# Issuing the last convolution, output weight and query stores on ScalarE's queue instead of SyncE's

## The chip, the cores and the metric

The kernel runs on one core of a Trainium2 chip. The metric is the time of one execution in microseconds, measured on the device; the median of several runs is quoted. The engines are named as in the profile: PE (TensorE matmul), PEld (TensorE weight load), DVE (VectorE), ACT (ScalarE), POOL (GpSimd), SP (SyncE, which only issues DMAs here; "SPq" in the rows). PEclk is the clock that TensorE was granted, as a share of 2.4 GHz.

## What is computed

One block of a hybrid encoder, in f32, on a sequence of 2048 rows of 1024 numbers. Cut to what matters here:

```python
xn = rms_norm(h, ln_mix_g)
proj = xn @ w_in                       # q, k, v, o, gates, c_q, c_kv, k_rope
qk = silu(dwconv3_centred(concat(q_pre, k_pre), conv_w, conv_b))
y_a = sigmoid(o_pre) * rms_norm(mlstm_fwd(qk, v, gates) + mlstm_bwd(qk, v, gates))
q = (rms_norm(c_q) @ w_uq)             # 4 heads: 128 plain and 64 rotated columns
o = softmax((q_nope @ k_nope.T + rope(q_rope) @ rope(k_rope).T) * scale) @ v
h = h + concat(y_a, y_b) @ w_out
h = h + conv_gated_mlp(rms_norm(h)); h = h + gate * rms_norm(p @ w_p)
out = rms_norm(h)
```

## The kernel before, in words

The kernel runs its stages one after another on a PE that is hardly ever without work; every intermediate goes to DRAM and comes back. All DMAs, loads and stores alike, are issued by SP, which works through one list in order: a DMA whose data are not ready holds up every DMA behind it. The framework gives each tile its semaphores and puts the instructions of each engine into an order of its own, by a simulated timetable in which program order is the priority; an instruction may therefore stand far ahead of the place where it is written. Only PE's order in the query stage is kept as written (`manual_schedule`).

Four stages matter, with their times in the profiled execution.

- **pairs** (to 424 us): `pairs()` runs 12 products, i = 0 to 11, each for two 128-column tiles of `w_in` and half the rows (`s.blk`), with seven partial products each (L544). `conv(s, half)` follows in the next iteration: for `s.pr` up to 3 it makes the depthwise convolution and Silu of a q or k tile and stores it to `qk_d`, else it makes the output gate and stores it to `o_d` (both stores are L576, 512 KB each). After i = 10 the corrected edge column is stored (L682). `queries_load` and `queries_begin` already fetch the next stage's weights during i = 10 and 11, among them the rotation tables of row blocks 0 and 1 (`load_table`, L749, tile `qcs`, tags t0 to t3).
- **queries** (424 to 482 us): `queries()` walks row blocks b = 0 to 3 of 512 rows. `rope(b)` makes two products `qpr`, rotates them on DVE (L815 to L817), splits the result into a high and a low part (`qso`: ACT casts, DVE subtracts) and stores it per head with four DMAs of 256 KB (L823). `latent(b, h)` makes the plain part of head h, ACT copies it to `qo` (L832), and one DMA stores it (L833). `weights(h)` folds a value weight into `w_out` (`woo`, copied by ACT at L799 and stored by two DMAs at L800). `split_c`, `split_wo` and `split_latent` make high and low parts of later operands (ACT casts, DVE subtracts). The tiles are reused: `qso` lies in two places by turns of b, `qo` in two by turns of head pairs, `woo` in two; so a copy into one waits until the earlier store from there has been read out.
- **attention's beginning**, woven into the queries: `attend_begin` loads the queries of the first 2 x 256 rows of head 0 back from `q_d` (`load_q`, L1162, tile `q_t`), splits them (ACT, then DVE), and starts the scores (L1155, tile `bk`, one PSUM bank for 512 keys, of which there are four that `rope`, `latent` and `weights` also use), the maximum (DVE L1184) and the exponential (ACT L1201). It is resumed at b = 1, 2 and 3.
- **attention and mLSTM** (482 to 1130 us) and then the MLP and gate stages (to the end), which the change does not touch.

The two lines that decide the order between queries and attention:

```python
if b == 1:
    att = self.attend_begin()
    next(att)                 # load_q(0, 0), load_q(0, 1)
if b > 1:
    next(att)                 # b = 2: split_q(0, 0)
```

Of the kernel before, what the change touches and what calls it, by code (L numbers as in the profile page):

```python
# [19 lines left out]
P = 128  # L20
# [15 lines left out]
SB = 512  # L36
# [12 lines left out]
def _f(ap):  # L49
    return ap.bitcast(F32)  # L50
# [10 lines left out]
class Block:  # L61
# [444 lines left out]
    def pairs(self):  # L506

        nc, d = self.nc, self.d
# [39 lines left out]
        def conv(s, half):  # L548
            u = s.u[half]
            if s.pr > 3:  # L550
                h = 2 * (s.pr - 4) + half
                nc.scalar.activation(u[:, 1 + SB:1 + 2 * SB], u[:, 1 + SB:1 + 2 * SB], AF.Sigmoid)
                t = self.at(("w7", "w11")[half], [P, 2 * SB], name="ct")
                nc.scalar.activation(t, u[:, 1:1 + 2 * SB], AF.Copy, scale=go[:, h:h + 1])
                dst = self.o_d[8 * s.blk:8 * s.blk + 8, :, h, :]
            else:
                ch = 2 * s.pr + half
                nc.vector.memset(u[:, 1 + 2 * SB:2 + 2 * SB], 0.0)
                if s.blk:
                    nc.vector.tensor_copy(u[:, 0:1], edge[:, ch:ch + 1])  # L560
                else:
                    nc.vector.memset(u[:, 0:1], 0.0)
                t = self.at(("w7", "w11")[half], [P, 2 * SB], name="ct")
                nc.scalar.activation(t, u[:, 0:2 * SB], AF.Identity, bias=cwt[:, 3, ch:ch + 1], scale=cwt[:, 0, ch:ch + 1])
                for tap in (1, 2):
                    nc.vector.scalar_tensor_tensor(t, u[:, tap:tap + 2 * SB], cwt[:, tap, ch:ch + 1], t,
                                                   op0=ALU.mult, op1=ALU.add)
                if s.blk:
                    nc.vector.scalar_tensor_tensor(part[:, ch:ch + 1], u[:, 1:2], cwt[:, 2, ch:ch + 1],
                                                   part[:, ch:ch + 1], op0=ALU.mult, op1=ALU.add)  # L570
                else:
                    nc.scalar.copy(edge[:, ch:ch + 1], u[:, 2 * SB:2 * SB + 1])
                    nc.scalar.copy(part[:, ch:ch + 1], t[:, 2 * SB - 1:2 * SB])
                nc.scalar.activation(t, t, AF.Silu)
                dst = self.qk_d[8 * s.blk:8 * s.blk + 8, :, ch, :]
            nc.sync.dma_start(dst.rearrange("c p t -> p c t"), t.rearrange("p (c t) -> p c t", t=P))  # L576

        def first_half(s, half, src):
            o = s.u[half][:, 1:1 + SB]
# [21 lines left out]
        for i in range(12):  # L601
            blk, j = divmod(i, 6)
            then = i == 5
            s = Pair()
            s.i, s.pr, s.blk, s.ops = i, j, blk, self.ops.pop(i)
            x, s.y = [self.pfa.tile([P, SB], F32, name=t, tag=t) for t in ("fx", "fy")]
            s.z, s.spare = [self.pfb.tile([P, SB], F32, name=t, tag=t) for t in ("fz", "fs")]
            s.u = [None, None]

            def side(at):  # L610
                if i == 0 and at == 1:
                    next(self.begun)
                if i == 0 and at in (2, 3):
                    for k in (2 * at - 4, 2 * at - 3):
                        self.xop["T3"][k] = self.in_place(0, "T3", k)
                        self.split(self.third[at - 2][:, k % 2], *self.xop["T3"][k])
                if i == 0 and at in (5, 6):
                    load("T4", range(2))
                if i == 1 and at in (1, 2):
                    load("B22", range(2))  # L620
                if (1, 4) < (i, at) < (5, 0) and at % 2:
                    self.gate_bank = prev.spare if at % 2 else s.spare
                    next(gates, None)
                if i == 11:
                    self.queries_begin(at, prev.spare if at % 2 else s.spare)

            if i < 2:
                op = self.xop["B11"][0]
                nc.tensor.matmul(s.y, s.ops["A11"][0][:, 0:P], op[0], start=True, stop=True)
            prod(x, s.ops["A11"], "B11")  # L630
            nc.scalar.copy(s.y, x)
            if then:
                load("B11")
            side(1)
            prod(s.z, s.ops["S1"], "T1")
            s.p5 = self.at("t6", [P, SB], name="p5")
            nc.scalar.copy(s.p5, s.z)
            if then:
                load("T1")
            side(2)  # L640
            if prev:
                rest_y(prev)
            if i == 6:
                load("T4")
            side(3)
            prod(s.y, s.ops["S2"], "T2", True)
            s.u[0] = self.at(next(urot), [P, 2 * SB + 2], name="ug")
            nc.scalar.copy(s.u[0][:, 1 + SB:1 + 2 * SB], s.y)
            if then:
                load("T2")  # L650
            side(4)
            if i + 1 < 12:
                for _ in self.pair_prep(i + 1):
                    pass
            if i + 2 < 12:
                self.pair_load(i + 2)
            if i == 10:
                self.queries_load()
            prod(x, s.ops["A12"], "B21", True)
            first_half(s, 0, x)  # L660
            side(5)
            if prev:
                rest_z(prev)
            if i == 6:
                load("B22")
            side(6)
            if then:
                load("B21")
            prod(s.y, s.ops["S3"], "T3", True)
            s.u[1] = self.at(next(urot), [P, 2 * SB + 2], name="uv")  # L670
            add(s.u[1][:, 1 + SB:1 + 2 * SB], s.p5, s.y)
            if then:
                load("T3")
            side(7)
            if i == 4:
                begin(1, self.NAMES)
            prev = s
            if i == 4:
                assert next(gates, 0) == 0
            if i == 10:  # L680
                nc.scalar.activation(part, part, AF.Silu)
                nc.sync.dma_start(self.qk_d[7, :, :, P - 1], part)  # L682
        rest_z(prev)
        rest_y(prev)

# [22 lines left out]
    def queries_begin(self, at, bank):  # L708

        nc = self.nc  # L710
        if at in (2, 4):
            kt = at // 2 - 1
            ps = bank.rearrange("p (h c) -> p h c", h=NH)
            for h in range(NH):
                nc.tensor.matmul(ps[:, h], self.uq[:, h, kt * P:(kt + 1) * P], self.uk[:, h], start=True, stop=True)
            nc.scalar.copy(self.wqr[kt][:, 0:512], bank)
        if at == 1:
            self.raws, self.tables = {}, {}
            self.first = self.at("x11", [P, 2, 2, SB], name="qraw")
            for b in range(2):  # L720
                self.load_latent(b)
                self.load_table(b)
        if at == 3:
            self.kraw = []
            for n in range(2):
                self.load_keys(n)
        if at == 5:
            self.wo = [self.split_wo(0)]
        if at == 6:
            self.kh, self.kl = self.split_latent(0, ("x12", "x13"))  # L730
# [36 lines left out]
    def queries(self):  # L767

        nc, d = self.nc, self.d
# [22 lines left out]
        def weights(h):  # L792
            (wh, wl), us = self.wo[h]
            for hf in range(2):
                fs = slice(hf * 512, hf * 512 + 512)
                ps = self.bank() if h else self.gbank()
                self.mm3(ps, us[:, 0], us[:, 1], wh[:, fs], wl[:, fs], True, True)
                o = self.at(("t6", "u2")[hf], [P, 512], name="woo")
                nc.scalar.copy(o, ps)  # L799
                nc.sync.dma_start(self.wo_d[h, :, fs], o)  # L800

        def product(ps, b, o):
            hi, lo = cc[b]
# [3 lines left out]
        def rope(b):  # L807
# [12 lines left out]
                self.split(t[2 * n], so[:, 0, n], so[:, 1, n])  # L820
            for h in range(NH):
                dst = self.q_d[h, 1, :, b * SB:(b + 1) * SB].rearrange("(a f) t -> f a t", a=4)
                nc.sync.dma_start(dst, _f(so[32 * h:32 * h + 32]).rearrange("p a n t -> p (a n) t"))  # L823
            if b < 2:
                self.load_table(b + 2)

        def latent(b, h):
            if h % 2 == 0:
                self.qo = self.at(f"u{h // 2}", [P, 2, SB], name="qo")
            ps = (self.bank if h % 2 and b < 3 else self.gbank)()  # L830
            product(ps, b, h * P)
            nc.scalar.activation(self.qo[:, h % 2], ps, AF.Copy, scale=ASCALE)  # L832
            nc.sync.dma_start(self.q_d[h, 0, :, b * SB:(b + 1) * SB], self.qo[:, h % 2])  # L833

        with self.tc.manual_schedule(engines={mybir.EngineType.PE}):
            split_wq()
# [1544 lines left out]
```

## Time and profile before

| | |
|---|---|
| median of 3 runs | 2837.93 us (2836.57 to 2844.72) |
| profiled execution, its own time | 2839.65 us |
| profiled execution, span first to last instruction | 2837.5 us |
| PE busy | 2803.8 us, 99% |
| DVE busy | 2123.0 us, 75% |
| ACT busy | 1573.2 us, 55% |
| DMA | 553.73 MB, mean 195 GB/s |

The span is what lies between the first and the last instruction of the profile; the execution's own time is 2.2 us longer. DMA-issuing instructions are in the timeline (SPq), with the time for which they occupied their queue, but are not counted as busy. The DMA share of a stretch is the mean busy share of the core's 16 DMA engines. A row of a timeline gives start, duration, engine, line, operation, tiles, count, and in brackets how long the engine had stood idle and on what. All DMAs of the kernel run on one queue, "q1 hardware_dynamic"; no row shows ACT issuing one.

### The profile page before, as it was taken

To read this page: it belongs to the slowest core of one execution; us is meant where nothing else is said; L and a number is where in the kernel's file an instruction comes from. 1 tells how busy PE (TensorE), PEld (TensorE's weight loads), DVE (VectorE), ACT (ScalarE), POOL (GpSimd) and SP (SyncE) were. 2 spreads that over 40 slices of the span, in tenths; PEclk is the share of its full clock that TensorE was granted. 3 is DMA by queue.
4 is the path that set the end of the run, shared out by engine and by line. 5 is a ranking of instruction groups with operands and counts; after the bars stand their busy time and mean duration, and the time that the engine had idled before them with its cause. 6 is when DMAs were issued, how large, how long until landed. Compare 5 with 4: busy or idle time off the path is not lost.

```text
span 2837.5 us, 39455 instructions
## 1 busy us (share of the span) xinstructions
PE 2803.8 (99%) x13756; PEld 2349.8 (83%) x13756; DVE 2123.0 (75%) x3597; ACT 1573.2 (55%) x3068; POOL 211.2 (7%) x331
## 2 busy tenths in 40 slices
PE   9999999999999999999999999999999999999998
PEld 8888887888888888888888888888888788888787
DVE  4867866778777777877778778777778766676777
ACT  6346775556565556655655556655556332254665
POOL 2100000000000000045100000000000000011012
PEclk9999999999999999999999999999999999999999
DMA  8874757654443333589645445567776757585864
GB/s 295 291 238 117 219 180 217 193 171 143 137 129 107 99 99 126 161 258 284 225 156 193 163 163 186 185 208 237 227 238 216 225 194 236 171 265 200 292 200 164
DMA packets 444207, 553.73 MB, mean 195 GB/s; under 512 B 34500, under 2 KB 294632, under 8 KB 444008
## 3 DMA queue, kind: packets, MB, share of 16 engines
q1 hardware_dynamic: 444008, 551.21, 60.2%
q8 instruction: 108, 1.77, 0.3%
q14 instruction: 91, 0.75, 0.1%
HBM read 358.50 MB, written 192.61 MB: 194 GB/s over the span
## 4 chain that ended last, share of the span: by engine, by line
PE 87%; DVE 4%; DMA 3%; ACT 1%; issue 1%; SPq 0%; POOL 0%; POOLq 0%; ACTq 0%; DVEq 0%
PE fy L1729 22%; PE fz L1729 15%; PE fx L1729 14%; PE bk L1155 9%; PE ppv L1236 6%; PE tb L1251 4%; PE fy L544 3%; PE bk L134 2%; PE fz L544 2%; PE fx L544 2%; PE fs L134 2%; PE mb L1117 1%; PE mb L1022 1%; PE mb L1118 1%; DMA opr<-tw_d 1%
## 5 line engine op out<-in xcount | busy, mean ns | idle before, releaser
L1729 PE MATMUL fz<-op,fw 128*128 128x512 f32 x1968 | 477.4, 391 | 2.7 <-DVE ug L1714 2.0
L1729 PE MATMUL fy<-op,fw 128*128 128x512 f32 x1968 | 475.2, 390 | 1.6 <-DVE xt L1714 1.6
L1729 PE MATMUL fx<-op,fw 128*128 128x512 f32 x1968 | 476.2, 390 | 0.0
L1729 PEld LDWEIGHTS fy<-op,fw 128*128 128x128 f32 x1968 | 368.6, 188 | 78.7 <-DVE xt L1714 2.0
L1729 PEld LDWEIGHTS fz<-op,fw 128*128 128x128 f32 x1968 | 367.4, 188 | 80.1 <-DVE ug L1714 2.5
L1729 PEld LDWEIGHTS fx<-op,fw 128*128 128x128 f32 x1968 | 368.1, 188 | 76.2
L1155 PE MATMUL bk<-kv,q_t 128*128 128x512 f32 x1280 | 337.4, 404 | 5.2 <-DVE q_t L124 4.0
L1155 PEld LDWEIGHTS bk<-kv,q_t 128*128 128x128 f32 x1280 | 230.3, 190 | 48.9 <-DVE q_t L124 4.4
L121 ACT CAST pt<-tb 128x512 fp32r<-128x512 f32 x256 | 139.7, 588 | 184.0 <-PE tb L1251 183.8
L1729 PE MATMUL fy<-op,fwd 128*128 128x512 f32 (+1 forms) x984 | 238.0, 390 | 2.5 <-DVE fh L1714 1.6
L1184 DVE TENSOR_REDUCE mx<-bk 128x1 f32<-128x512 f32 x256 | 174.8, 686 | 60.7 <-PE bk L1155 57.9
L1729 PEld LDWEIGHTS fy<-op,fwd 128*128 128x128 f32 x984 | 182.6, 188 | 41.5 <-DVE fh L1714 1.9
L1236 PE MATMUL ppv<-pt,kv 128*128 128x512 f32 (+1 forms) x1024 | 198.7, 344 | 1.0 <-DVE pt L124 1.0
L1201 ACT ACTIVATE pe<-bk,nm 128x512 f32<-128x512 f32 x256 | 174.2, 697 | 36.7 <-DVE nm L1195 36.4
L124 DVE TENSOR_TENSOR pt<-tb,pt 128x512 fp32r<-128x512 f32 x256 | 167.8, 684 | 32.3 <-ACT pt L121 30.5
L124 DVE TENSOR_TENSOR fw<-fwr,fw 128x1024 fp32r<-128x1024 f32 x124 | 150.9, 1220 | 34.5 <-ACT fw L121 34.3
L1236 PEld LDWEIGHTS ppv<-pt,kv 128*128 128x128 f32 x1024 | 156.0, 189 | 20.4 <-DVE pt L124 1.5
L121 ACT CAST op<-opr 128x512 fp32r<-128x512 f32 x201 | 116.9, 618 | 74.4 <-DMA opr<-tw_d 13.3
L121 ACT CAST fw<-fwr 128x1024 fp32r<-128x1024 f32 x124 | 129.8, 1051 | 37.4 <-DVE fwr L1703 20.2
L124 DVE TENSOR_TENSOR op<-opr,op 128x512 fp32r<-128x512 f32 x201 | 131.5, 690 | 25.4 <-ACT op L121 23.8
L1251 PE MATMUL tb<-ident,pe 128*128 128x128 f32 x1024 | 135.2, 273 | 0.1
L121 ACT CAST fw<-hraw 128x1024 fp32r<-128x1024 f32 (+1 forms) x72 | 70.1, 980 | 114.7 <-PE fx L1729 59.1
(397 smaller groups left out, 4443.2 us busy)
## 6 DMA issues: line engine op xcount, KB each, us to landing
fwr<-in_w_up SPq DMA_DIRECT2D x66, 512.0 KB, 4.9
fh<-h_d SPq DMA_DIRECT2D x48, 512.0 KB, 4.1
h_d<-fh SPq DMA_DIRECT2D x48, 512.0 KB, 4.5
s_d<-fwr SPq DMA_DIRECT2D x44, 512.0 KB, 3.4
fws<-s_d SPq DMA_DIRECT2D x44, 512.0 KB, 3.6
rw<-row_d SPq DMA_DIRECT2D x32, 512.0 KB, 4.9
tw_d<-tsum SPq DMA_DIRECT2D x60, 256.0 KB, 5.3
opr<-tw_d SPq DMA_DIRECT2D x60, 256.0 KB, 4.4
```

The source lines that it names most:

```text
L121: nc.scalar.copy(hi, src)
L124: (sub or nc.vector).tensor_tensor(lo, src, _f(hi), op=ALU.subtract)
L134: mm = lambda *a, **k: self.nc.tensor.matmul(*a, **k, skip_group_check=more)
L544: nc.tensor.matmul(out, a[:, k * P:(k + 1) * P], parts[lo], start=first, stop=lo == 1 and k == 3, skip_group_check=more)
L1022: mm(ps[:, i, 0:129], kw[:, h, :], v1[:, h, :], start=True, stop=True)
L1117: mm(ps[:, i, 0:129], mk2[:, r, h, :], v1[:, h, :], start=True, stop=False)
L1155: mm = lambda *a, **k: self.chained(nc.tensor.matmul(*a, **k))
L1184: nc.vector.tensor_reduce(s.mx[:, kb:kb + 1], ps, axis=AX.X, op=ALU.max)
L1201: nc.scalar.activation(s.pe[:, kb % 2], s.banks[kb], AF.Exp, bias=s.nm, accum_out=s.rs[:, kb:kb + 1])
L1236: mm = lambda *a, **k: self.chained(nc.tensor.matmul(*a, **k))
L1251: self.chained(nc.tensor.transpose(t[:, j, :], s.p[kb][:, j * P:(j + 1) * P], self.ident))
L1729: nc.tensor.matmul(out, a[:, k * P:(k + 1) * P], parts[lo][:, cols], start=first, stop=lo == 1 and k == last, skip_group_check=more)
```

## The change

The stores of `conv` for i = 9, 10 and 11 (six), the edge column's store, the eight stores of `woo`, the sixteen of `qso` and the sixteen of `qo` are issued by ACT, 47 in all; everything else stays with SP. The loads of the first two rotation tables are written at i = 9 instead of in `queries_begin` at i = 11.

```diff
@@ conv @@
-            nc.sync.dma_start(dst.rearrange("c p t -> p c t"), t.rearrange("p (c t) -> p c t", t=P))
+            issue = nc.scalar if s.i > 8 else nc.sync
+            issue.dma_start(dst.rearrange("c p t -> p c t"), t.rearrange("p (c t) -> p c t", t=P))
@@ pairs @@
             if i + 2 < 12:
                 self.pair_load(i + 2)
+            if i == 9:
+                self.raws, self.tables = {}, {}
+                for b in range(2):
+                    self.load_table(b)
...
                 nc.scalar.activation(part, part, AF.Silu)
-                nc.sync.dma_start(self.qk_d[7, :, :, P - 1], part)
+                nc.scalar.dma_start(self.qk_d[7, :, :, P - 1], part)
@@ queries_begin @@
         if at == 1:
-            self.raws, self.tables = {}, {}
             self.first = self.at("x11", [P, 2, 2, SB], name="qraw")
             for b in range(2):
                 self.load_latent(b)
-                self.load_table(b)
@@ queries: weights, rope, latent @@
-                nc.sync.dma_start(self.wo_d[h, :, fs], o)
+                nc.scalar.dma_start(self.wo_d[h, :, fs], o)
...
-                nc.sync.dma_start(dst, _f(so[32 * h:32 * h + 32]).rearrange("p a n t -> p (a n) t"))
+                nc.scalar.dma_start(dst, _f(so[32 * h:32 * h + 32]).rearrange("p a n t -> p (a n) t"))
...
-            nc.sync.dma_start(self.q_d[h, 0, :, b * SB:(b + 1) * SB], self.qo[:, h % 2])
+            nc.scalar.dma_start(self.q_d[h, 0, :, b * SB:(b + 1) * SB], self.qo[:, h % 2])
```

## Rows read from the trace of the kernel before

**Rows 1.** The page, part 1: busy time of each engine.

```profile
PE 2803.8 (99%) x13756; PEld 2349.8 (83%) x13756; DVE 2123.0 (75%) x3597; ACT 1573.2 (55%) x3068; POOL 211.2 (7%) x331
```

**Rows 2.** Waits of PE, whole span: total us, times, longest.

```profile
PE bk L1155 <- DVE q_t L124: 4.0, 1, 4.0
PE mb L1022 <- DVE kk L1015: 2.3, 1, 2.3
...
PE bk L1155 <- ACT pe L1201: 1.2, 2, 1.0
```

**Rows 3.** Busy by stretch; after ACT and POOL: granted clock, DMA share, GB/s.

```profile
454.00:458.00 4.00, 0.62 (x3) 0.19 (x1) 0.00 (x0) 2.86 (x7) 0.00 (x0) 0.90 1.03 341
458.00:460.00 2.00, 1.35 (x3) 1.16 (x4) 0.76 (x2) 0.44 (x2) 0.00 (x0) 0.50 1.02 339
...
462.00:464.00 2.00, 2.00 (x7) 1.52 (x6) 0.68 (x1) 0.00 (x0) 0.00 (x0) 0.50 0.99 382
...
507.00:510.00 3.00, 0.69 (x6) 0.66 (x6) 2.56 (x5) 1.28 (x3) 0.00 (x0) 1.00 0.80 272
```

**Rows 4.** Chain that ended last, in order of time, ahead of the first scores.

```profile
451.97 4.68 DMA q_d<-qo
...
457.84 0.30 ACT q_t L121
458.17 0.44 DVE q_t L124
```

**Rows 5.** Timeline of SP's queue, around the query loads and later.

```profile
448.46 0.91 SPq L833 DMA_DIRECT2D q_d<-qo  x2
...
451.49 1.01 SPq L833 DMA_DIRECT2D q_d<-qo  x2
452.58 1.47 SPq L1162 DMA_DIRECT2D q_t<-q_d  x2
454.15 3.62 SPq L823 DMA_DIRECT2D q_d<-qso  x4
...
472.98 2.80 SPq L823 DMA_DIRECT2D q_d<-qso  x4
475.88 2.94 SPq L833 DMA_DIRECT2D q_d<-qo  x3
```

**Rows 6.** Issues by tile: duration ns min/median/max, first and last start.

```profile
L800 SPq DMA_DIRECT2D wo_d<-woo x8: 382/522/1099, 427.1 to 460.4; - x8
L833 SPq DMA_DIRECT2D q_d<-qo x16: 319/680/1185, 430.1 to 480.9; - x16
L823 SPq DMA_DIRECT2D q_d<-qso x16: 319/530/1878, 436.1 to 474.5; - x16
```

**Rows 7.** ACT by stretch: length, busy, granted clock, DMA share, GB/s.

```profile
424.00:443.30 19.30, 18.17 (x31) 1.00 0.99 314
443.30:449.80 6.50, 0.02 (x1) 1.00 0.86 196
449.80:458.50 8.70, 5.88 (x12) 0.93 1.01 346
458.50:467.00 8.50, 0.00 (x0) 0.67 0.67 241
```

**Rows 8.** Timeline of ACT: copies and casts that waited for stores.

```profile
449.78 1.18 ACT L121 CAST qso<-qtt 128x512 fp32r<-128x512 f32 x2 [6.51 <-DMA q_d<-qso]
...
453.57 0.60 ACT L832 ACTIVATE qo<-gb 128x512 f32<-128x512 f32 x1 [1.62 <-DMA q_d<-qo]
...
456.76 0.60 ACT L832 ACTIVATE qo<-gb 128x512 f32<-128x512 f32 x1 [1.14 <-DMA q_d<-qo]
```

**Rows 9.** Timeline of ACT, first cast of the attention's probabilities.

```profile
475.57 0.59 ACT L121 CAST pt<-tb 128x512 fp32r<-128x512 f32 x1 [2.66 <-PE tb L1251]
```

**Rows 10.** Timeline of SP's queue: the first rotation tables.

```profile
325.09 3.19 SPq L749 DMA_DIRECT2D qcs<-in_rope_queries  x4
```

**Rows 11.** Timeline of DVE ahead of the cast at 449.78.

```profile
449.02 0.68 DVE L816 TENSOR_TENSOR qtt<-qtt 128x512 f32<-128x512 f32 x1
```

## The prediction

> **What bounds the kernel now.** I read the page's busy times first. PE is at work for 99% of the span and ACT for 55% [rows 1], so a store that moves can pay only where PE stands still. The list of PE's waits over the whole span says where: the three that lie near the change are 4.0 us for the split of the first queries, 2.3 us for a key product and 1.2 us for an exponential [rows 2]. The rest are at the start or after the attention. The largest wait of the kernel is thus the one at which attention begins, and the change moves the stores in front of it.
>
> The stretches put a second price on that wait. PE is almost empty from 454 to 458; from 458 the granted clock is 0.50, the lower of the two levels (1.2 GHz), and stays there in three stretches of 2 us, up to 464 [rows 3]. PE's pause at 507 to 510, 2.3 us long, did not lower the clock: it stayed at 1.00 [rows 2, 3].
>
> The chain says what PE waited for: a DMA of `qo` to `q_d` that ended at 456.7, ACT's next copies, then the query split on ACT at 457.84 and on DVE at 458.17 [rows 4]. PE starts at 458.17 + 0.44 = 458.6 and so had nothing to do from 454.6. Two things made that late. On SP, the query loads were issued at 452.58, behind stores of `qo` at 448.46 and 451.49 [rows 5], though they read only row block 0, stored long before. On ACT, copies into `qo` stood still for 1.62 and 1.14 us because the earlier stores from there were not read out [rows 8]. One row misleads: the cast at 449.78 is put down to a DMA, after 6.51 us of idleness [rows 8], but its input left DVE only at 449.02 + 0.68 = 449.70 [rows 11]. That idle time is ACT waiting for PE's products; faster stores do not remove it, though it is room.
>
> **The change part by part.** 47 issues leave SP for ACT: 5 before 424 us, 24 between 424 and 449.8 (2 of `o_d`, 6 of `woo`, 8 of `qso`, 8 of `qo`, counting the last two copies of block 1 where PE has made them ready), 10 of block 2, 8 of block 3.
>
> *What can be won.* The wait of 4.0 us, and the half clock from 458.6 to 464.0, 5.4 x 0.5 = 2.7 us: 6.7 us in all, no more, unless the 2.3 and 1.2 us vanish too. SP comes as far as the `qo` stores at 448.46; without them it can issue the query loads there: 448.5 + 1.5 for the two issues + 4.7, the landing time of the DMA in the chain, = 454.7 [rows 4, 5]. The data are then in place about when PE runs out. The writes into `qo` no longer wait on SP's list, so the 1.62 + 1.14 = 2.8 us on ACT mostly go.
>
> *What it costs.* ACT must now issue. No row shows an issue on ACT, so I bound it by SP's. The shortest is 0.32 us [rows 6]. With a full queue they are longer: 0.91 and 1.01 for two each, 3.62 and 2.80 for four, 2.94 for three [rows 5], 11.28 us for 15, 0.75 each. Below 0.32 nothing speaks for a price; a gain by the issue itself is excluded, since ACT did not issue before. For `qso` I take 0.70, from the set at 472.98 (2.80 for four), which came long after the set at 454.15 [rows 5] and is the nearest to an unhurried one; for `qo`, `woo` and `o_d` 0.40, near the lower end, since on ACT their copies lie between them. For the 24 that is 8 x 0.70 + 16 x 0.40 = 12.0 us (ends 7.7 and 18.0). ACT's free time there is 1.13 + 6.48 = 7.6 us [rows 7]. ACT is therefore 12.0 - 7.6 = 4.4 us late at 449.8 (ends 0.1 and 10.4).
>
> The query split, when its data are in place, stands behind the two casts of block 2's `qso` (1.18 us [rows 8]) and perhaps behind their four stores (2.8). 449.8 + 4.4 + 1.2 = 455.4, and with 0.8 for the split on ACT and DVE 456.2; behind the stores, 459.0. The order on ACT is the framework's and not to be read from the diff. I take 457.0, nearer the lower, since these stores must first wait for DVE's half. PE's gap is then 2.4 us, like the one at 507 that left the clock alone [rows 2, 3]. Won: 4.0 - 2.4 + 2.7 = 4.3 us.
>
> Two things are given back. The scores use the banks that ACT frees by copying `woo` and `qo`, and ACT is late: between 0 and its lag of 4.4 us, and 1.5 is taken, since PE needs one bank at a time and each group of scores gives ACT time. The 8.5 us in which ACT now does nothing, 458.5 to 467.0 [rows 7], absorb what is left, so the debt ends there. In block 3, four `qso` and two `qo` stores (2.80 + 2 x 0.98 = 4.8 us) fall into 2.66 us of ACT's idleness before the probability cast at 475.57 [rows 5, 9]: 2.1 us too many, on a path where PE already waits 1.2 us for an exponential. Ends 0 and 2.1; I take 0.8.
>
> Costed at nothing: the 5 earlier stores, some 2 us of ACT, spread over 30 us of the pairs in which PE waits for nobody; if ACT were late there, the copy of `fx` would hold PE. The table loads: written at i = 11, they are issued at 325.09, during i = 6 [rows 10], so writing them at i = 9 changes nothing but a priority.
>
> *The sum.* -4.3 + 1.5 + 0.8 = -2.0 us: 2839.65 - 2.0 = 2837.65 for an execution like the profiled one, which was 1.7 us above the median of 2837.93. For the median: 2836.0.
>
> One rule speaks against the change. DMAs keep 0.99 of the 16 engines busy from 424 to 443 and 1.01 from 449.8 to 458.5 [rows 7]; only 443 to 449.8 has room, at 0.86. The Trainium skill, "DMA: Bandwidth & Descriptors", section "Issuing engines are not separate DMA queues", says that DMAs run on the same 16 engines whoever issues them, and that issuing from several saves only the sequencer's time. By that rule the stores land no sooner and the sum is that of the second rival below; the rows say the same of the stores, but not of the loads' place in the line.
>
> **The rivals.**
>
> *ACT becomes the bound (slower).* Place: ACT's list from 424 to 458. For: it has 18.17 us of work in 19.3 [rows 7] and gets at least 7.7 more; a store that finds the queue full stops all copies and splits behind it. Against: 8.5 us of idleness follow at once, and ACT's stores have copies between them. It decides from a lag of 4.0 us (split behind the stores) or 6.8 us (ahead of them), which is (7.6 + 4.0) / 24 = 0.48 or 0.60 us per store; I took 0.50, so it is close. At 0.75: 449.8 + 10.4 + 1.2 + 2.8 + 0.8 = 465.0, 6.4 us later than now, with 2 for banks and 2.1 in block 3 = +10.5: 2848.4. At 0.62 it is half of that, about 2843.
>
> *The transfers are the bound (no change).* For: the shares above. The loads trade places with stores, the `qo` places come free no sooner, and what the loads win, ACT's copies lose. Also here: the framework's order keeps the query split last, behind all of block 2, and nothing is seen of the freed SP. Time 2838.
>
> *Everything closes.* ACT's issues cost 0.32, the lag is 0.1, attention starts without a gap, and the shifted start also dissolves the 2.3 and 1.2 us: -6.7 - 3.5 = -10.2, 2827.7. Against: the 2.3 us at 507 hang on a key product behind SP's other work, which isn't touched.
>
> **How the numbers follow.** Forecast 0.50 (own range 2831 to 2838), ACT bound 0.27, transfers bound 0.15, everything 0.08. About 0.3%, 8.5 us, is what a measurement of this kernel can tell from no change. Faster by more needs nearly all of the last rival: 0.07. Slower by more needs a price near 0.7 us: 0.12. The rest, 0.81, is within. The range runs from 2829.5, past the full 6.7 us and short of the last rival, to 2846, most of the way to the price of 0.75.
>
> **What would show it.** Right: the query loads issued before 450; PE's gap near 455 under 2.5 us, clock 1.00 from 458 to 464; ACT busy or issuing without a break from 424 to about 455, little idleness at 443 to 450. Wrong: issues on ACT of 0.6 us and more, PE waits for ACT's copies (banks) between 435 and 455; a query split still at 458 or later; a clock of 0.50 after it. If PE's waits elsewhere, in the attention or the MLP, change by microseconds, the framework has reordered more than the diff says, and the sum fails for that.

## The result, and the profile after

The changed kernel takes 2854.64 us (median of six runs, 2853.56 to 2855.69), the kernel before 2838.11 beside it: 1.0057 times as long, 95% interval 1.0047 to 1.0067. It is slower by 16.5 us; 2836.0 was forecast, with 2846.0 as the upper end. The profiled execution took 2853.98 us, its span is 2852.2, 14.7 more than before.

The page of the kernel after, parts 1 and 3 (busy time of each engine; queue, kind, packets, MB, share of 16 engines):

```profile
PE 2806.7 (98%) x13756; PEld 2350.8 (82%) x13756; DVE 2122.7 (74%) x3597; ACT 1574.5 (55%) x3068; POOL 214.3 (8%) x331
...
q1 hardware_dynamic: 430968, 537.57, 58.2%
q10 hardware_dynamic: 13040, 13.64, 1.6%
```

Beside [rows 1] PE is busy for 2.9 us more, at the same number of matmuls, so that is a lower clock; the other 11.8 us of the span are PE standing still. A second hardware queue, q10, carries the 13.64 MB that ACT now issues. The change does what it says.

PE's waits in the kernel after (total, times, longest), those from 424 to 500 us:

```profile
PE bk L1158 <- DVE q_t L124: 7.1, 1, 7.1
PE bk L134 <- DVE uvs L124: 5.7, 2, 5.5
PE mb L1013 <- DMA kTb<-qk_d: 4.5, 1, 4.5
...
PE bk L134 <- DVE qtt L818: 1.6, 1, 1.6
...
PE qpr L134 <- DVE qtt L818: 1.4, 1, 1.4
```

The wait of 4.0 us for the first query split [rows 2] has not gone but grown to 7.1. Ahead of it stand new waits of 5.5, 1.6 and 1.4 us, behind it one of 4.5 for the first keys. The 2.3 and 1.2 us of [rows 2] are gone.

The stretch that shows it best runs from PE's first product for `woo` to its first score. It holds the same 133 or 134 matmuls in every kernel here. The kernel before, then the kernel after with the 10 us that follow (columns as in [rows 3]: PE, PEld, DVE, ACT, POOL, clock, DMA share, GB/s):

```profile
423.58:458.65 35.07, 30.62 (x134) 24.53 (x132) 24.44 (x41) 24.49 (x43) 0.00 (x0) 0.98 0.97 300
```

```profile
424.58:475.34 50.76, 34.29 (x133) 25.46 (x131) 26.85 (x41) 25.95 (x44) 0.00 (x0) 0.90 0.79 237
...
475.40:485.00 9.60, 9.60 (x35) 7.77 (x36) 6.67 (x12) 4.46 (x12) 0.00 (x0) 0.81 0.29 107
```

The stretch grew from 35.1 to 50.8 us, by 15.7; the whole span of the profiled execution grew by 14.7, so this stretch holds the loss. PE idles in it for 16.5 us instead of 4.5, and it is at work for 3.7 us more, as its clock sinks to 0.90. The DMA share **fell** from 0.97 to 0.79, so it is not the throughput of the transfers that PE waits for.

Issues by tile after (ns, shortest, median, longest), the lines that answer to [rows 6]:

```profile
L803 ACTq DMA_DIRECT2D wo_d<-woo x8: 326/346/1827, 429.0 to 474.0; - x8
...
L836 ACTq DMA_DIRECT2D q_d<-qo x16: 326/340/1140, 437.0 to 502.2; - x16
...
L826 ACTq DMA_DIRECT2D q_d<-qso x16: 310/462/1812, 437.5 to 493.3; - x16
```

Summed over the stretch from the timeline, ACT's 32 issues take 18.7 us, 0.58 each (12 of `qso` at 0.73, 20 others at 0.50). They may not simply be added to ACT's 25.95 us of work, because an issue can run while ACT's last copy is still at work; here the first starts 0.13 us after a copy:

```profile
457.22 0.59 ACT L835 ACTIVATE qo<-bk 128x512 f32<-128x512 f32 x1
457.35 0.86 ACTq L836 DMA_DIRECT2D q_d<-qo  x2
```

In this way 4.1 of the 18.7 us lie beside work. Counted once, work and issues cover 40.6 of the 50.8 us, against 24.5 of 35.1 before. In the other 10.2 us ACT neither works nor issues; before, these were 10.6. So the stretch grew by what was put on ACT, and ACT's free time took in next to nothing of it. Three pieces make 8.9 of the 10.2 us: 1.1 at the start, 3.0 for DVE's first rotated queries, and the largest, 4.9, in ACT's timeline:

```profile
437.51 2.93 ACTq L826 DMA_DIRECT2D q_d<-qso  x4
...
442.39 5.80 ACTq L803 DMA_DIRECT2D wo_d<-woo  x2
448.23 1.04 ACT L121 CAST woa<-wor 128x1024 fp32r<-128x1024 f32 x1 [5.38 <-DMA qcs<-in_rope_queries]
...
452.83 2.81 ACTq L826 DMA_DIRECT2D q_d<-qso  x4
455.69 1.14 ACT L121 CAST kv<-kvr 128x512 fp32r<-128x512 f32 x2 [2.74 <-issue]
...
474.43 0.40 ACT L121 CAST q_t<-q_t 128x256 fp32r<-128x256 f32 x1 [0.42 <-ACT woo L802]
```

The second of two `woo` stores at 442.39 was issued only at 447.86. It stood 4.9 us for the landing of a rotation table (`qcs`), with which it has nothing in common. The instruction lists say why: here the framework gives a DMA one of eight completion semaphores, DMAHW0 to DMAHW7, whichever of SP and ACT issues it, and it waits until the last user of that semaphore has landed. These two have the same one (in the trace's operands both raise number 105, and ACT waits for 105 just ahead of the store).

```
ACT: 403 L803 DMA wo_d_91<-woo_4049 128x512 [waits DMAHW3_49,Activation_49]
SP:  286 L752 DMA qcs_4114<-in_rope_queries 128x512 [waits DMAHW3_49,DVE_49]
```

While SP issued every DMA, such a wait followed the order in which it worked anyway. Now ACT stands for SP's load, and that load had to wait for DVE. SP's queue and the chain of waits of the kernel after:

```profile
442.98 0.95 SPq L752 DMA_DIRECT2D qcs<-in_rope_queries  x2
444.10 0.96 SPq L1165 DMA_DIRECT2D q_t<-q_d  x2
```

```profile
442.98 4.80 DMA qcs<-in_rope_queries
447.86 0.33 ACTq L803
...
452.95 0.21 ACTq L826
453.20 0.45 ACTq L826
453.68 0.68 ACTq L826
454.40 1.24 ACTq L826
...
474.03 0.35 ACTq L803
474.43 0.41 ACT q_t L121
474.86 0.44 DVE q_t L124
...
475.34 4.72 PE bk L1158 x12
```

The query loads are issued at 444.10, 8.5 us earlier than in [rows 5]; the freed SP did its part. But from 447.86 to 474.84 every step of the chain is ACT, its issues among them, and the query split comes at 474.43, behind the copies and stores of block 2.

### The profile page after: what moved, and what is told of

The parts are those of the page before. It is cut to its first block, busy times and chain, and to the rows that moved or that the text cites. A ratio compares the mean times of both kernels' runs of the same rounds, so it can differ in the third digit from the quotient of the medians.

```text
span 2852.2 us, 39443 instructions
## 1 busy us (share of the span) xinstructions
PE 2806.7 (98%) x13756; PEld 2350.8 (82%) x13756; DVE 2122.7 (74%) x3597; ACT 1574.5 (55%) x3068; POOL 214.3 (8%) x331
## 3 DMA queue, kind: packets, MB, share of 16 engines
q10 hardware_dynamic: 13040, 13.64, 1.6%
## 4 chain that ended last, share of the span: by engine, by line
PE 85%; DMA 4%; DVE 4%; ACT 2%; issue 2%; SPq 1%; POOL 0%; ACTq 0%; POOLq 0%; DVEq 0%
PE fy L1732 22%; PE fz L1732 15%; PE fx L1732 14%; PE bk L1158 10%; PE ppv L1239 6%; PE tb L1254 4%; PE bk L134 2%; PE fy L544 2%; PE fx L544 2%; PE fs L134 2%; PE fz L544 1%; PE mb L1120 1%; PE mb L1025 1%; PE mb L1121 1%; DVE op L124 1%
## 5 line engine op out<-in xcount | busy, mean ns | idle before, releaser
L1732 PE MATMUL fy<-op,fw 128*128 128x512 f32 x1968 | 475.3, 390 | 1.4 <-DVE xt L1717 1.4
L1732 PEld LDWEIGHTS fy<-op,fwd 128*128 128x128 f32 x984 | 182.6, 188 | 40.5 <-DVE fh L1717 1.8
L121 ACT CAST op<-opr 128x512 fp32r<-128x512 f32 x201 | 117.5, 618 | 77.8 <-DMA opr<-tw_d 14.7
L124 DVE TENSOR_TENSOR op<-opr,op 128x512 fp32r<-128x512 f32 x201 | 131.5, 692 | 24.9 <-ACT op L121 24.3
```

Source lines behind the costliest of these rows:

```text
L121: nc.scalar.copy(hi, src)
L124: (sub or nc.vector).tensor_tensor(lo, src, _f(hi), op=ALU.subtract)
L1732: nc.tensor.matmul(out, a[:, k * P:(k + 1) * P], parts[lo][:, cols], start=first, stop=lo == 1 and k == last, skip_group_check=more)
```

## The experiments

**The four parts alone**, each put into the kernel before.

```diff
# conv_alone
+            (nc.scalar if s.i > 8 else nc.sync).dma_start(dst.rearrange("c p t -> p c t"), ...
+                nc.scalar.dma_start(self.qk_d[7, :, :, P - 1], part)
# rope_alone
+                nc.scalar.dma_start(dst, _f(so[32 * h:32 * h + 32]).rearrange("p a n t -> p (a n) t"))
# plain_alone
+            nc.scalar.dma_start(self.q_d[h, 0, :, b * SB:(b + 1) * SB], self.qo[:, h % 2])
# weights_alone
+                nc.scalar.dma_start(self.wo_d[h, :, fs], o)
```

> The kernel before with only the six last convolution stores and the edge store issued on ScalarE; everything else on SyncE, table loads as before. The changed kernel loses 16.5 us. Theory 1 (ScalarE pays for the issue itself): 7 issues of about 0.4 us, 3 us of ScalarE in a stretch with room: within 1 us of before. Theory 2 (a DMA on one queue waits, through a completion semaphore that both queues share in turn, for an unrelated DMA of the other queue): few meetings of the two queues, 0 to +3 us. Theory 3 (the framework puts the first query split last on ScalarE's list only when the other stores are there): 0.

> The kernel before with only the sixteen stores of the rotated queries (qso) on ScalarE. Their issues took about 3 us for each set of four in the changed kernel, 13.7 us in all. Theory 1: these are over half of the issue time, so over half of the loss, +8 to +10 us. Theory 2: the loss goes with the number of places where the queues take turns, about a third of it: +4 to +6 us, seen as ScalarE standing between issues for longer than the issues last. Theory 3: the plain query and weight stores stay on SyncE, so the query load is still behind them and the split still late: about 0.

> The kernel before with only the sixteen stores of the plain queries (qo) on ScalarE, issues of about 0.4 us each. Theory 1: 6 us of ScalarE's time, a quarter of the loss or less, 0 to +4 us. Theory 2: stores wait for the rotated stores and the table loads of SyncE eight places earlier: +4 to +8 us. Theory 3: the query load is no longer behind them, and if the split is early on ScalarE's list the time is 3 to 6 us below before.

> The kernel before with only the eight stores of the output weights (woo) on ScalarE. Theory 1: 8 issues of 0.35 us, 3 us: 0 to +1 us. Theory 2: one of them stood 5.4 us for a table load in the changed kernel; if that comes back, +2 to +5 us. Theory 3: 0.

Beside 2838.91 for the kernel before: conv_alone 2842.74 (ratio 1.0011, 1.0002 to 1.0021), rope_alone 2841.55 (1.0010, 1.0001 to 1.0020), plain_alone 2837.36 (0.9999, 0.9989 to 1.0008), weights_alone 2839.89 (1.0006, 0.9996 to 1.0015). The differences of the medians are +3.8, +2.6, -1.5 and +1.0; they add to 6, and the whole costs 16.5. The last two are not told apart from no change. By the medians no theory fits all four: the `qso` stores, which theory 1 makes over half of the loss and theory 2 a third, cost 2.6, and conv_alone lies above all three. With intervals of some 2.7 us to either side the four decide little. Weights_alone, PE's wait at the first scores, and rope_alone, ACT's `qso` sets ahead of them:

```profile
PE bk L1155 <- DVE q_t L124: 9.6, 1, 9.6
```

```profile
436.27 5.36 ACTq L823 DMA_DIRECT2D q_d<-qso  x4
444.01 4.66 ACTq L823 DMA_DIRECT2D q_d<-qso  x4
454.34 4.60 ACTq L823 DMA_DIRECT2D q_d<-qso  x4
```

Of the 14.6 us of these three sets only 8.7 are issues; for the rest ACT stands between them. Each part lengthens the stretch to the first score (by 2.7 to 5.6 us), yet the end hardly moves: weights_alone waits 9.6 us there instead of 4.0, without the 2.3 us that follow in [rows 2] and with 0.7 of the 1.2. So a few microseconds at that place are given back, as forecast; 15.7 are not.

**The same stores on an idle queue.** All 47 on GpSimd instead of ACT:

```diff
-                nc.scalar.dma_start(...)
+                nc.gpsimd.dma_start(...)        # all 47
```

> The changed kernel with the 47 stores on GpSimd's queue instead of ScalarE's: SyncE is freed of them as in the change, ScalarE issues nothing, and GpSimd has no other work here. Theory 1 and theory 2 both expect most of the loss to go: 2832 to 2840, at or below before. If freeing SyncE itself were what hurts (its loads in other places, the transfers in another order), the time stays above 2846.

2841.85 beside 2838.86 (1.0011, 1.0002 to 1.0021), above the 2832 to 2840 that were expected, but far below 2846. That leaves 16.5 - 3.0, some 13 us, to the fact that ACT issues. That nothing is won either says that a freed SP alone is worth nothing here: PE no longer waits for the query split, but 5.8 us for the first keys (`kTb`) and 2.9 for rotated queries.

**Only the query loads leave SP's list.** The kernel before, with the first two `load_q` on GpSimd:

```diff
-            nc.sync.dma_start(_f(q[:, 0:2]), self.q_d[h, :, ...
+            (nc.gpsimd if h == 0 and pr < 2 else nc.sync).dma_start(_f(q[:, 0:2]), self.q_d[h, :, ...
```

> The kernel before, all 47 stores on SyncE, but the first two query loads (512 KB together) go over GpSimd's queue, past SyncE's list. The forecast of the change held that these loads stood behind stores. If that place in the list is what makes PE wait 4.0 us and run 5.4 us at the half clock: 3 to 6.7 us below before, 2832 to 2835. If ScalarE's list or the landing of the stores is what ends last: within 1 us of before.

**2832.07** beside 2838.86 (0.9978, 0.9969 to 0.9987): 6.8 us faster than before, and the fastest of all. Its timelines of POOL and ACT, then the stretches of [rows 3]:

```profile
440.79 1.66 POOL L1162 DMA_DIRECT2D q_t<-q_d  x2 [261.22 <-DMA q_d<-qso]
...
446.56 0.41 ACT L121 CAST q_t<-q_t 128x256 fp32r<-128x256 f32 x1 [2.94 <-DMA q_t<-q_d]
```

```profile
458.00:460.00 2.00, 2.00 (x11) 1.65 (x10) 1.11 (x3) 0.42 (x1) 0.00 (x0) 1.00 0.97 243
460.00:464.00 4.00, 4.00 (x20) 3.30 (x19) 2.97 (x6) 2.00 (x6) 0.00 (x0) 1.00 1.00 316
```

The split runs at 446.56, PE does not wait for it, and the clock that was 0.50 [rows 3] is 1.00. With the tables of row blocks 2 and 3 on GpSimd too, the median lies between the two:

```diff
-            self.nc.sync.dma_start(t[e], self.d["rope_queries"][...
+            (self.nc.gpsimd if b > 1 else self.nc.sync).dma_start(t[e], self.d["rope_queries"][...
```

> The kernel before, all stores on SyncE, with the first two query loads and the rotation tables of blocks 2 and 3 over GpSimd's queue. The query loads alone gave 2832.1. The table loads take 2 us of SyncE's list between rope stores and query stores; if the copies into qo still wait for those stores (0.66 us there), 0 to 2 us more: 2830 to 2832. If not, the same as the query loads alone.

2835.11 beside 2838.43 (0.9987, 0.9978 to 0.9997). The 2830 to 2832 that were expected were missed; the intervals of the two kernels overlap, so it is not shown that the tables' place costs anything.

**One cure at a time for the changed kernel**: the first query splits on DVE (`act=h > 0 or pr > 1` in `split_q`); the tables on GpSimd, by the diff above; the 16 `qso` stores on GpSimd; then two pairs of these.

> The changed kernel (2854.6 us), but the high part of the first two query tiles is copied by VectorE instead of ScalarE, so that the query split is no longer on ScalarE's list. Their data were asked for at 444.1 in the changed kernel and split at 474.4. Theory 1 (issue time on ScalarE) and theory 3 (place of the split on ScalarE's list): attention begins up to 10 us earlier, PE's wait of 7.1 us for it shrinks below 2: 2844 to 2850. Theory 2 (waits of one queue for DMAs of the other through shared semaphores): ScalarE is as late as before and the scores' banks with it; PE waits for banks instead: 2851 to 2856.

> The changed kernel, but the rotation tables of row blocks 2 and 3 are loaded over GpSimd's queue, which has completion semaphores of its own; all 47 stores stay on ScalarE. In the changed kernel one store of the output weights stood on ScalarE from 443.0 to 447.9 until a table load of SyncE had landed. Theory 2: that stand is gone, PE's wait of 5.5 us behind it (for the weight split) too: 5 to 9 us below the changed kernel, 2845 to 2850. Theory 1: the same issues on ScalarE, the same time within 2 us. Theory 3: the same within 2 us unless the order changes.

> The changed kernel with the sixteen stores of the rotated queries (qso) on GpSimd's queue and the other 31 still on ScalarE. Between the changed kernel (2854.6) and the one with all 47 on GpSimd (2841.9) lie 12.7 us. Theory 1 (issue time on ScalarE): three sets of four cost 9 of some 20 us of issuing before attention begins, and block 3's set 4.6 more; 5 to 8 us come back, 2846 to 2850. Theory 2 (stands of one queue for the other's DMAs through shared semaphores): the stand for the table load stays, 2851 to 2854. Theory 3 (place of the query split): stays last, 2850 or more, with PE's wait for it still over 4 us.

> The changed kernel with both single cures together: the first two query splits copied by VectorE, and the tables of blocks 2 and 3 loaded over GpSimd's queue. Alone they gave 3.8 and 2.8 us. If the stand (theory 2) and the place of the split (theory 3) were what costs, together 6.5 us or more, 2848 or below. If ScalarE's issue time (theory 1) is the bound behind both, less than their sum: PE waits for banks that ScalarE's copies free, 2848 to 2852.

> The changed kernel with the first two query splits copied by VectorE and the rotated queries' stores on GpSimd's queue. Theory 1 and theory 3 together: the two largest parts of the loss are gone, 2841 to 2846, near the kernel with all stores on GpSimd. Theory 2: the stand for the table load is left, PE still waits about 5 us for the weight split behind it, 2848 or above.

In this order: 2850.89 (1.0040, 1.0026 to 1.0055), 2851.85 (1.0047, 1.0032 to 1.0062), 2850.86 (1.0042, 1.0028 to 1.0057), 2851.09 (1.0039, 1.0025 to 1.0054), 2850.99 (1.0041, 1.0026 to 1.0056). Each cure is worth about 4 us, and two are worth no more than one; with four or five runs each, the intervals reach some 4 us to either side, so the five are not told apart. PE's waits with the split on DVE, and ACT's `woo` pair with the tables on GpSimd:

```profile
PE bk L134 <- DVE uvs L124: 6.4, 1, 6.4
PE mb L1013 <- DMA kTb<-qk_d: 5.0, 1, 5.0
PE bk L1158 <- ACT qo L835: 3.7, 1, 3.7
```

```profile
443.48 1.65 ACTq L803 DMA_DIRECT2D wo_d<-woo  x2
```

With the split off ACT, PE waits at the same scores for another copy of ACT, a bank behind `qo`. (The 6.4 us come earlier, and DVE has a part in them: the split that was moved there stood 4.1 us for its load, with `uvs` behind it.) With the table off SP's hardware queue the pair that took 5.80 us takes 1.65, which bears the shared semaphore out; yet the wait for the split is still 6.4 us.

**What is it in ACT's issuing?** Three kernels: all stores on GpSimd, but ACT loses the time of an issue ahead of each of 40; the changed kernel without the loads for which ACT stood; three cures at once.

```diff
# pool_stores_act_held: as stores_on_pool, and ahead of each store of woo, qso, qo
+                nc.scalar.copy(o[:, 0:480], o[:, 0:480])
# after_loads_on_pool: as after, with both GpSimd diffs above (first two load_q, tables b > 1)
# after_three_cures: as after, split on DVE, tables b > 1 and qso stores on GpSimd
```

> All 47 stores on GpSimd's queue as in stores_on_pool, but ahead of each of the 40 stores of woo, qso and qo ACT copies 480 columns of the stored tile onto themselves, about 0.55 us each: ACT loses the time that the issues took in the changed kernel (0.58 us each), without standing for the semaphores of other DMAs. If the lost time of ACT alone makes the loss (theory A): 2851 to 2856, as the changed kernel's 2854.6. If standing for unrelated transfers makes most of it (theory B): 2842 to 2847, near stores_on_pool's 2841.9. Between 2847 and 2851: both, in about equal parts.

> The changed kernel with the two query loads and the rotation tables of row blocks 2 and 3 on GpSimd's queue: ACT still issues all 47 stores, but no longer stands for these loads, which caused its stands of 4.9 and 4.1 us. Theory A (ACT's time): 2849 to 2852, like after_tables_on_pool's 2851.9, with the 18.7 us of issues between 424 and 475 unchanged and the query split still behind block 2. Theory B (standing): 2840 to 2846.

> The changed kernel with the first query splits on DVE, the tables of row blocks 2 and 3 and the 16 qso stores on GpSimd's queue; ACT keeps 31 issues of 0.3 to 0.5 us, some 9 us between 424 and 475 instead of 18.7. If ACT's list is the bound and each cure alone only uncovers the next stand (theory A), the three together give more than any pair: 2843 to 2848. If the loss is one that no cure so far has touched (PE's new order, the kTb load): 2849 to 2852 again.

Beside 2839.11: 2844.84 (1.0019, 1.0009 to 1.0028), 2853.91 (1.0057, 1.0040 to 1.0074), 2846.10 (1.0027, 1.0017 to 1.0038). The stretch to the first score in each, in the same order:

```profile
423.66:463.12 39.46, 33.30 (x134) 25.36 (x132) 24.62 (x40) 36.45 (x66) 16.13 (x28) 0.96 0.81 251
```

```profile
425.08:473.45 48.37, 34.72 (x133) 26.08 (x131) 26.51 (x41) 26.02 (x44) 3.85 (x6) 0.90 0.79 249
```

```profile
423.91:467.09 43.18, 33.58 (x134) 25.80 (x132) 26.98 (x44) 23.94 (x39) 8.50 (x16) 0.92 0.80 238
```

What ACT did in that stretch (with two kernels that come below), from these rows and the issues of each timeline (us; in brackets the issues or the copies that stand for them; "neither" counts an issue beside a copy once, so the columns of a kernel with issues add to more than its stretch; the time by difference of the medians to the kernel before beside it):

| kernel | stretch | ACT's own work | issues or holds | neither | time |
|---|---|---|---|---|---|
| before | 35.1 | 24.5 | - | 10.6 | 0 |
| before_queries_on_pool | 32.5 | 23.1 | - | 9.4 | -6.8 |
| stores_on_pool | 36.5 | 23.4 | - | 13.1 | +3.0 |
| pool_stores_act_held | 39.5 | 20.4 | 16.0 (27) | 3.0 | +5.7 |
| after_three_cures | 43.2 | 23.9 | 9.8 (18) | 13.0 | +7.0 |
| after_split_forward_loads_pool | 44.2 | 24.5 | 16.8 (30) | 7.2 | +12.9 |
| after_split_on_dve | 47.0 | 24.0 | 17.3 (30) | 10.0 | +12.0 |
| after_split_forward | 47.9 | 24.3 | 18.4 (30) | 9.5 | +14.4 |
| after_loads_on_pool | 48.4 | 26.0 | 19.4 (32) | 6.9 | +14.8 |
| after | 50.8 | 26.0 | 18.7 (32) | 10.2 | +16.5 |

Neither theory came out whole. Lost time by itself is the lesser part: with holds of 0.59 us each ACT is busy for 36.45 of 39.46 us, as full as it can be, and the kernel loses only 2.7 us more than stores_on_pool, which is within the noise. Standing for the loads is not the rest: without it (6.9 us of neither instead of 10.2) after_loads_on_pool still loses 14.8. The stretches of these two differ by 8.9 us. Of that, 5.0 are the list ahead of the first scores: 20.4 us of copies and 27 stores' worth with the holds, 26.0 and 32 with real issues (36.45 and 41.5 us, counted once). The other 3.9 are ACT doing neither. The split of the first queries runs at 454.37 in the one and at 474.43 in the changed kernel. So the last two kernels put the split forward in ACT's list and leave every store on ACT, the second without the loads for which ACT stood:

```diff
         load_q(0, 1)
+        split_q(0, 0)
         yield
-        split_q(0, 0)
         yield
# after_split_forward: as after, with this; after_split_forward_loads_pool: as after_loads_on_pool, with this
```

> The changed kernel with split_q(0, 0) written right behind its load at b = 1: in ACT's list it now stands ahead of block 2's qso casts and all their stores; all 47 stores stay on ACT. If the place of the split is what the loss comes from, the wait for it at the first scores (7.1 us in the changed kernel) goes, nothing takes its place, and the time is 2844 to 2848, near pool_stores_act_held. If ACT's list as a whole holds PE (its banks and casts behind stores), another wait appears, and it is 2850 to 2852 as with the split on DVE.

> The same with the two query loads and the tables of row blocks 2 and 3 on GpSimd's queue, so that ACT no longer stands for them. If place and standing are together the difference to pool_stores_act_held (2844.8): 2843 to 2847. If the issues on ACT hold PE in another way: 2849 to 2853.

Beside 2838.28: 2852.70 (1.0049, 1.0034 to 1.0063) and 2851.16 (1.0041, 1.0027 to 1.0056). PE's waits in the first, and in the second the stretch:

```profile
PE bk L134 <- DVE uvs L124: 5.6, 2, 5.4
PE bk L1158 <- ACT qo L835: 4.3, 1, 4.3
PE mb L1013 <- DMA kTb<-qk_d: 4.3, 1, 4.3
```

```profile
425.42:469.58 44.16, 33.80 (x133) 25.23 (x131) 26.37 (x41) 24.45 (x40) 3.86 (x6) 0.95 0.78 249
```

The wait for the split is gone, and at the same scores PE waits 4.3 us for ACT's copies into `qo`, which free the banks. That is the second branch of the expectation: not the place of one instruction but **ACT's list as a whole** holds PE. The chain of waits of after_split_forward bears it out: from 446.0 to the first score at 470.74 every step of it is ACT or one of its issues. The scores are written behind block 2's products, so they need block 2's copies as well as the split; every copy stands behind the stores ahead of it, and whichever is brought forward, the next takes its place. The single cures, which give 2 to 4 us, fit this.

The kernels with the split on DVE measure something else as well. In DVE's list the split stands until the query loads have landed, and holds up what is behind it. PE's longest wait in after_split_dve_rope_pool and in after_three_cures, and DVE's timeline in the latter:

```profile
PE qpr L134 <- DVE cq L124: 10.5, 1, 10.5
```

```profile
PE qpr L134 <- DVE cq L124: 6.9, 1, 6.9
```

```profile
450.38 0.29 DVE L123 CAST q_t<-q_t 128x256 fp32r<-128x256 f32 x1 [6.65 <-DMA q_t<-q_d]
```

PE's next operand, `cq`, is split on DVE behind the queries. So what these two kernels lose is not ACT's list alone: in after_three_cures ACT does neither for 13.0 of 43.2 us. That the pair with `qso` gives no more than one cure has this cause at least in part; three cures, with half of the issue time, do better in spite of it.

What stays open: pool_stores_act_held has as much on ACT's list in all as the changed kernel, but the framework puts some 4 to 6 us less of ACT's own work ahead of the first scores; why it orders ACT differently when ACT does not issue was not found. The chains of after_three_cures and after_split_dve_rope_pool show a query load with 9.68 and 10.98 us, and 18 issues take 9.8 us in the one and 14.8 in the other; neither was followed up. The rotation tables written at i = 9 were not tried by themselves, but the trace shows no sign of them: the first four are issued at 326.00 instead of 325.09 [rows 10].

## Why the prediction was wrong

**The ceiling was right.** 4.0 us of waiting and 2.7 of half clock were to be won; before_queries_on_pool wins 6.8, with clock 1.00 and no wait for the split. That it is so near 6.7 is in part luck: its interval reaches from 3.7 to 8.8, and the 2.3 us of [rows 2], not in that sum, are gone as well. That it was SP's list which held the query loads was right too: 8.5 us earlier in the changed kernel.

**The price was nearly right.** 0.70 for `qso` and 0.40 for the others were taken, 0.73 and 0.50 measured; for the 32 issues 16.4 by the forecast, 18.7 in fact: 2.3 us short. As 4.1 of these lie beside copies, ACT paid 14.6. In the parts by themselves `qso` cost 0.73 (12 in 8.73), `woo` 0.49, `qo` 0.35. What was costed at nothing held as far as the traces show: the table loads moved by 0.9 us, and ahead of the stretch PE waits for 0.7 us more. The +3.8 of conv_alone, whose stretch begins at 422.94, must come later; it was not followed up.

**The step that failed** is "The query split, when its data are in place, stands behind the two casts of block 2's `qso` (1.18 us [rows 8]) and perhaps behind their four stores (2.8) ... I take 457.0". It counts 1.2 us of block 2, at most 4.0, as lying ahead of the first scores; "behind all of block 2" stood only under a rival, at a price of nothing. All of block 2 lies ahead of them: in the changed kernel the split itself stands there, and in after_split_forward, where it does not, the `qo` copies hold PE instead. [Rows 7] could have told it: ACT works 5.88 us from 449.8 to 458.5 and then stops, just as the scores begin. By the forecast's own terms that gives 449.8 + 4.4 + 5.9 (block 2's copies) + 4.4 (its eight stores ahead of the split) + 0.8 = 465.3. PE started at 475.34. So of the 18.3 us between 457.0 and 475.3, this step is 8.3. The other 10.0 are not the price: from 424.0, the forecast's list with all of block 2 is 40.5 us of work and issues, and 40.6 were measured. They are time in which ACT stood.

**The banks** were to cost 1.5, "since PE needs one bank at a time", with 4.4 as the upper end. Where the split is out of the way and all stores are on ACT, the wait for them is 3.6 to 4.3 us: the upper end. With the `qso` stores on GpSimd as well it is 0.9 and 1.1.

**The term that was missing** is that standing. "ACT's free time there is 1.13 + 6.48 = 7.6 us" was taken off the price of the issues, as if they could fill it. They did not: ACT stands for 10.2 us in the changed kernel and for 10.6 before. Nearly half is new in kind: stores and loads on two queues share completion semaphores, so a store on ACT can wait for a load on SP. No row of before shows such a wait, and the forecast had none between the queues. In the changed kernel it is 4.9 us in one place; with the tables away, 1.65 us are left of that pair's 5.80. In row block 3 the same holds `qo` stores for a query load:

```profile
493.96 4.81 ACTq L836 DMA_DIRECT2D q_d<-qo  x2
498.81 1.07 ACT L121 CAST pt<-tb 128x512 fp32r<-128x512 f32 x2 [9.47 <-DMA q_t<-q_d]
```

By itself the standing decides little, as after_loads_on_pool shows.

**"The 8.5 us in which ACT now does nothing ... absorb what is left"**: they came too late. They lie behind the first scores, and the scores waited. Also given back later were only the 2.3 and 1.2 us; a new wait of 4.5 for `kTb` takes their place, which stores_on_pool (5.8) and rope_alone (4.2) have too.

**The rivals.** "ACT becomes the bound" was the right mechanism. Its point of decision, 0.48 to 0.60 per store, is met by the length of an issue (0.58) but not by what an issue took from ACT beside its copies (0.46, 14.6 us over 32). By its formula 0.58 gives some 2841, and its worst case is 2848.4; block 2's whole list and the standing lay outside it. "The transfers are the bound" fell: the DMA share went down to 0.79 while all became slower. The Trainium skill, "DMA: Bandwidth & Descriptors", section "Issuing engines are not separate DMA queues", has it that issuing from several engines saves only the time of initiating a DMA, usually small beside the DMA itself. The trace agrees as to one DMA: 0.58 us on ACT, beside 3.5 (`qo`) and 4.1 (`qso`) from issue to landing. But moved to an engine with copies of its own, that time was 18.7 us of a stretch of 50.8.

## What to carry to other kernels

Before moving DMAs to a compute engine's queue, write down what that engine must do ahead of the next thing that PE waits for, with the issues in the list, every copy that frees a bank among them. PE goes on no earlier than that whole sum allows, wherever the one instruction stands. Do not count the engine's free time as room for the issues unless it is clear what it waits for there. The same holds for a cure: an instruction moved to another engine makes that engine stand for the same data. If a load is late behind stores, move the load to an idle queue, not the stores to a busy one: two loads on GpSimd gave -6.8 us, 47 stores on ACT +16.5. After moving DMAs to a second queue, look in the instruction lists for completion semaphores that both queues share.

## What the runs showed that was not expected

- A store stood 4.9 us for an unrelated load on another engine's queue; the pair took 5.80 us, and 1.65 or 1.03 once those loads were on GpSimd.
- The four issues of one `qso` set on ACT grow in a row: 0.33, 0.45, 0.68, 1.24 us (the chain above counts 0.21 of the first). The three sets ahead of the scores take 2.8 to 3.4 us each in the changed kernel, and 4.6 to 5.4 where SP keeps all other stores (rope_alone), there with 5.9 us of standing in all three.
- An ACT that is at work for 92% of a stretch (36.45 of 39.46 us) cost less than one that works or issues for 80% (40.6 of 50.76 us).
- A split moved from ACT to DVE made DVE stand 6.65 us for its load, and PE 6.9 us for what came behind it.
